# A hybrid decoder trunk on one Trainium2 core: score matmuls of sparse attention issued for both query tiles at once

## Chip, cores and metric

The kernel runs on one core of a Trainium2 chip. The metric is the device time of one execution in microseconds (us), as the median of several runs. One profiled execution gives the trace that is read below; its times count from the start of its span.

## What is computed

Input and output are 256 tokens by 1024 features, float32. The trunk has two layers. Each is a token mixer behind an RMS norm, a residual add, and a squared-ReLU MLP. The change concerns only the mixer of layer 1, native sparse attention with 16 heads in 4 groups of 4. It has three branches with keys and values of their own: compressed, selected blocks, sliding window. With 256 tokens every block is selected and the window holds the whole past, so the last two are plain causal attention. Cut to what matters:

```python
def nsa_mixer(h, w_in, cmp_pos_k, cmp_k_w1, cmp_k_w2, cmp_pos_v, ..., w_out):
    q, kc, vc, ks, vs, kw, vw, g = jnp.split(h @ w_in, cuts, axis=-1)
    kc = compress(kc, cmp_pos_k, cmp_k_w1, cmp_k_w2)   # 15 blocks: gelu(flat @ w1) @ w2
    vc = compress(vc, cmp_pos_v, cmp_v_w1, cmp_v_w2)
    ...
        pc = jax.nn.softmax(sc, axis=-1)     # compressed, sc = q.kc*scale - slope*dist
        ps = jax.nn.softmax(ss, axis=-1)     # selected
        pw = jax.nn.softmax(sw, axis=-1)     # window
        out = g0 * (pc @ vc) + g1 * (ps @ vs) + g2 * (pw @ vw)
    return out @ w_out
```

## The kernel before

All 256 tokens are two query tiles `t` of 128. A float32 projection is written as three products of rounded halves (`wh`/`wl` of the weights, `x1h`/`x1l` of the input): `fmajor_steps` issues 8 x 3 matmuls of the full 128x128 array into one PSUM bank, for the keys (`ps_k`), the queries of a group (`ps_q`) and the inputs of the compression (`ps_c`). ScalarE casts each weight block into `wh` (L66), VectorE forms `wl` (L69). The banks of these products, of transposes (`pt`, `ptc`) and of products with values (`o`) come from one set of four that is used in turn.

Score matmuls are smaller: `nsa_scores(g, t, b)` (L947) issues four, one for each head of group `g`, for one query tile and branch `b` (0 selected, 1 window), each on a 64x128 part of the array, into a tile `s` of two banks; there are two such tiles, and the compressed scores use them too. Behind each set of matmuls follows its softmax: VectorE adds the distances and takes the extreme (L964), ScalarE takes the exponential with its sum (L967), VectorE inverts and gates the sums (L969, L970), GpSimd scales (L972). `nsa_cmp_scores(g)` (L974) does the compressed branch of a group with eight small matmuls, its adds on VectorE at L987. `values(i)` transposes the probabilities of one group and tile; `products(i)` multiplies them by the values (`o`, parts of 128x64). `compress_hidden` (`ps_h`, also 128x64) and `compress_gelu` (copy `hc` at L886, then `ps_hT`) are the MLP of the compression.

The order is written as Python generators: `run(a, b)` steps through several of them in proportion, so that a set of scores falls between the steps of a projection. A scheduler then fixes the queue of each engine, with the order of the program as priority; on the chip each queue runs in order. The mixer goes: keys `ks`, queries of group 0, keys `kw` beside the scores (0, 0), compression input of the keys beside the scores (0, 1), that of the values, then queries, hidden layers and the scores (1, 0) and (1, 1), and then for each group and tile transposes, products, scores of the groups 2 and 3, and the projections that are left. Out of `kw` come the copies `kd` (L709 on ScalarE, L710 on VectorE), and out of `ps_c` the copies `fsk` and `fsv` (L866 and L868), four on each engine for each bank.

Of the kernel before, what the change touches and what calls it, by code (L numbers as in the profile page):

```python
# [85 lines left out]
class Trunk:  # L86
# [577 lines left out]
    def odd_mixer(self, xT, oT, pool, out):  # L664
        nc = self.nc

        v2 = pool.tile([P, 2, 2, NG * 64], F32, name="v2")

        gates = pool.tile([P, 3, 2, 16], F32, name="gates")

        kd = pool.tile([P, NG, KW], F32, name="kd")

        vc = pool.tile([P, NG, 2, 64], F32, name="vc")
        pc = [pool.tile([P, 2, 2, 2, 32], F32, name=f"pc{i}") for i in range(2)]
        self.nsa_constants(pool)
        nc.gpsimd.memset(kd[:, :, CW - 1 : CW], 0.0)
        nc.gpsimd.memset(vc, 0.0)
        for z in pc:
            nc.gpsimd.memset(z, 0.0)
        ws = self.W.get(("vs",))  # L680
        w0 = self.W.get(("vw", 0))
        w1 = self.W.get(("vw", 1))
        for t in range(2):
            if t:
                self.run_late()
            ps = self.bankB("ps_vs")
            self.tmajor(ps[:, :S], ws, xT, t, range(8), True, True)
            nc.scalar.copy(v2[:, t, 0, :], ps[:, :S])
            ps = self.bankB("ps_vw")
            self.tmajor(ps[:, :304], w0, xT, t, range(4), True, False)  # L690
            self.tmajor(ps[:, :304], w1, xT, t, range(4, 8), False, True)
            nc.vector.tensor_copy(v2[:, t, 1, :], ps[:, :S])
            ga = gates[:, :, t, :]
            nc.scalar.activation(ga, ps[:, 256:304].rearrange("p (h b) -> p b h", b=3), AF.Exp, scale=-1.0)
            nc.vector.tensor_scalar(ga, ga, 1.0, None, op0=ALU.add)
            nc.vector.reciprocal(ga, ga)
        g0 = gates[:, 0, 0, :]
        nc.vector.tensor_scalar(g0, g0, self.valid, None, op0=ALU.mult)

        def keys(key, off):  # L700
            yield 2 * KT
            w = self.W.get((key,))
            for m in range(2):
                ps = self.bankB("ps_k")
                yield from self.fmajor_steps(ps[:, :S], w, m, xT)
                for i in range(2):
                    src = ps[64 * i : 64 * i + 64, :S]
                    c = slice(off, off + S)
                    nc.scalar.copy(kd[64 * i : 64 * i + 64, 2 * m + i, c], src)  # L709
                    nc.vector.tensor_copy(kd[64 - 64 * i : 128 - 64 * i, 2 * m + i, c], src)  # L710
                yield 1

        with self.tc.tile_pool(name="nsa", bufs=1) as up, \
                self.tc.tile_pool(name="ps_nsa", bufs=2, space=PSUM) as banks:
            qs, p, parts = {}, {}, {}

            def queries(g):
                return self.nsa_queries(g, xT, qs, up)

            def scores(g, b):  # L720

                yield 2
                for t in range(2):
                    self.nsa_scores(g, t, b, qs, kd, gates, p, up, banks)
                    yield 1

            def cmp_scores(g):
                self.nsa_cmp_scores(g, qs, kd, gates, pc[g % 2], banks)

            order = [(g, t) for g in range(NG) for t in range(2)]  # L730

            def values(i):

                g, t = order[i]
                todo = self.nsa_transposes(g, t, p, pc[g % 2], parts, up)
                yield next(todo)
                for n, _ in enumerate(todo):
                    if n == 0 and i > 0:
                        products(i - 1)
                    yield 1  # L740

            def products(i):
                g, t = order[i]
                self.nsa_products(g, t, parts, oT, v2, vc)

            run(keys("ks", CW))
            run(queries(0))
            run(keys("kw", CW + S), scores(0, 0))
            f = [None, None]
            run(self.compress_blocks(0, xT, up, pool, f), scores(0, 1))  # L750
            run(self.compress_blocks(1, xT, up, pool, f))
            q1 = queries(1)
            next(q1)
            run(part(q1, KT))
            h = [self.bankB(f"ps_h{kv}") for kv in range(2)]
            run(self.compress_hidden(f[0], h[0]))
            hk = self.compress_gelu(0, h[0], up)
            run(part(q1, KT))
            run(self.compress_hidden(f[1], h[1]), scores(1, 0))
            hv = self.compress_gelu(1, h[1], up)  # L760
            self.compress_keys(hk, f[0], kd)
            q2 = queries(2)
            next(q2)
            run(part(q2, KT), scores(1, 1))
            self.compress_values(hv, f[1], vc)
            cmp_scores(0)
            run(part(q2, KT), values(0))
            cmp_scores(1)
            q3 = queries(3)
            next(q3)  # L770


            run(values(1), part(q3, 4))
            run(values(2), part(q3, 6), scores(2, 0))
            run(values(3), part(q3, 6), scores(2, 1))
            cmp_scores(2)
            rows = self.out_rows("odo", oT)
            next(values4 := values(4))
            run(part(values4, 1))
            run(part(values4, 2), part(rows, 2), scores(3, 0))  # L780
            run(values(5), part(rows, 2), scores(3, 1))
            cmp_scores(3)
            run(values(6), part(rows, 2))
            run(values(7), part(rows, 2))
            products(7)
            return out(banks)
# [155 lines left out]
    def nsa_scores(self, g, t, b, qs, kd, gates, p, pool, banks):  # L942


        nc = self.nc
        n = P * (t + 1)
        if t:  # L947
            o = self.scratch(pool, [P, 4, n], "p")
        else:
            if b == 0:  # L950
                p[g] = self.tmp.tile([P, 2, 4, n], F32, tag=("xg", "gain")[g % 2], name="p")
            o = p[g][:, b]
        p[g, t, b] = o
        nm = self.sm.tile([P, 4], F32, tag="nm", name="nm")
        sums = self.sm.tile([P, 4], F32, tag="sums", name="sums")
        c0 = CW + b * S
        ps = banks.tile([P, 1024], F32, tag="s2", name=f"s{g}{t}{b}")
        z = [ps[:, h % 2 * 512 + h // 2 * n : h % 2 * 512 + h // 2 * n + n] for h in range(4)]
        for h in range(4):
            d = slice(64 * (h % 2), 64 * (h % 2) + 64)  # L960
            self.mm(z[h], qs[g][d, h // 2, t * P : (t + 1) * P], kd[d, g, c0 : c0 + n], True, True,
                    skip_group_check=True)
        for h in range(4):
            nc.vector.tensor_tensor_reduce(out=o[:, h], in0=z[h], in1=self.dist[:, 2 * P - n : 2 * P], op0=ALU.add,  # L964
                                           op1=ALU.min, scale=-self.slope(4 * g + h), scalar=BIG,
                                           accum_out=nm[:, h : h + 1])
            nc.scalar.activation(o[:, h], o[:, h], AF.Exp, bias=nm[:, h : h + 1], scale=-1.0,  # L967
                                 accum_out=sums[:, h : h + 1])
        nc.vector.reciprocal(sums, sums)  # L969
        nc.vector.tensor_mul(sums, sums, gates[:, 1 + b, t, 4 * g : 4 * g + 4])  # L970
        for h in range(4):
            nc.gpsimd.tensor_scalar(o[:, h], o[:, h], sums[:, h : h + 1], 0.0, op0=ALU.mult, op1=ALU.add)  # L972

    def nsa_cmp_scores(self, g, qs, kd, gates, pc, banks):  # L974
# [3 lines left out]
        for t in range(2):  # L978
            for a in range(2):
                for r in range(2):  # L980
                    d = slice(64 * r, 64 * r + 64)
                    i = 2 * t + a
                    self.mm(ps[:, r, i * CW : (i + 1) * CW], qs[g][d, a, t * P : (t + 1) * P], kd[d, g, :CW], True, True,
                            skip_group_check=True)
        for t in range(2):
            dist = self.dist[:, 2 * P + t * CW : 2 * P + (t + 1) * CW]
            nc.vector.tensor_add(pc[:, t, :, :, :CW], ps[:, :, 2 * t * CW : 2 * (t + 1) * CW].rearrange("p r (a c) -> p r a c", a=2),  # L987
                                 bass.AP(tensor=dist.tensor, offset=dist.offset, ap=[dist.ap[0], [0, 2], [0, 2], [1, CW]]))
# [171 lines left out]
```

## Time and profile before

| what | value |
|---|---|
| median of 3 runs (666.63, 667.12, 1045.58) | 667.12 us |
| profiled execution, its own time | 669.41 us |
| its span, from first to last instruction | 667.7 us |
| mean granted TensorE clock in it | 0.985 |
| busy share: TensorE, VectorE, ScalarE, GpSimd | 97, 61, 52, 7 % |

The mixer of layer 1 takes the stretch from about 345 to 475 us. In the timeline each line is one instruction, or several alike in a row (xN): its start, its time, engine, line, operation, the tile it writes and those it reads, and in brackets how long the engine had been idle before it and which instruction of which engine released it. A float32 matmul of the scores runs in two passes, so four of them are x8. The array part of a matmul stands before its shape: 128*128 is the full array. Matmuls overlap, so the pitch from one start to the next is what one costs, not its own time.

### The profile page before, as it was taken

The page shows a single profiled execution, that of the slowest core. Times are in us where ns is not written, and L with a number is a line of the kernel's source. Part 1 is how long each engine was busy: PE and PEld are TensorE (multiplying, and loading weights), DVE is VectorE, ACT ScalarE, POOL GpSimd, SP SyncE. Part 2 cuts the span into 40 slices and gives each one's busy share as a digit, 9 for nine tenths or more (in the row PEclk, how much of TensorE's full clock was granted, in tenths as well). Part 3 has the DMA queues.
Part 4 walks back from the last instruction along what each step waited for, and adds up shares of the span by engine and source line. Part 5 has one row for each costly group of instructions (what it writes and reads, how often), then busy time and mean ns, then how long its engine had stood idle before and what let it go on. Part 6 is the DMA issues. An engine that isn't in the chain of part 4 may idle for free.

```text
span 667.7 us, 11136 instructions
## 1 busy us (share of the span) xinstructions
PE 647.5 (97%) x4257; PEld 566.6 (85%) x4257; DVE 408.4 (61%) x820; ACT 346.7 (52%) x699; POOL 46.3 (7%) x139
## 2 busy tenths in 40 slices
PE   6899999999999999999999989999999999999995
PEld 3798898889989898988898878777899899998984
DVE  5854637886555555555877485776775555555534
ACT  5565556555444444444567464753554445454423
POOL 3200000000000000000203321430000000000000
PEclk7999899999999999999999999999999999999998
DMA  7784243346555555555597632023365555656601
GB/s 255 229 261 138 71 149 127 116 156 212 188 183 189 182 182 183 184 186 143 155 319 243 194 110 64 1 64 124 110 222 180 188 188 190 189 190 185 192 2 63
DMA packets 74277, 108.67 MB, mean 163 GB/s; under 512 B 5072, under 2 KB 60400, under 8 KB 74224
## 3 DMA queue, kind: packets, MB, share of 16 engines
q1 hardware_dynamic: 74224, 107.97, 50.6%
q8 instruction: 33, 0.54, 0.3%
q14 instruction: 20, 0.16, 0.1%
HBM read 106.91 MB, written 1.05 MB: 162 GB/s over the span
## 4 chain that ended last, share of the span: by engine, by line
PE 90%; DVE 5%; ACT 2%; issue 1%; DMA 1%; SPq 0%; ACTq 0%; DVEq 0%
PE macc L108 26%; PE ps_up L108 24%; PE ps_f L108 7%; PE acc L108 4%; PE ps_q L108 4%; PE ps_ut L108 3%; PE ps_v L108 3%; PE o L108 2%; PE s L108 2%; PE z L108 2%; PE ps_or L108 2%; PE ps_k L108 2%; PE pt L1015 2%; DVE wl L69 1%; PE ps_h L108 1%
## 5 line engine op out<-in xcount | busy, mean ns | idle before, releaser
L69 DVE TENSOR_TENSOR wl<-w,wh 128x1024 fp32r<-128x1024 f32 (+1 forms) x188 | 225.1, 1214 | 176.8 <-ACT wh L66 176.5
L66 ACT CAST wh<-w 128x1024 fp32r<-128x1024 f32 (+1 forms) x190 | 192.9, 1040 | 176.0 <-PE macc L108 83.3
L108 PE MATMUL macc<-wh,l 128*128 128x512 f32 x256 | 101.2, 395 | 0.0
L108 PE MATMUL macc<-wh,h 128*128 128x512 f32 x256 | 101.1, 395 | 0.0
L108 PE MATMUL macc<-wl,h 128*128 128x512 f32 x256 | 101.0, 394 | 0.0
L108 PE MATMUL ps_up<-m0h,wh 128*128 128x256 f32 x224 | 63.4, 283 | 0.0
L108 PE MATMUL ps_up<-m1h,wh 128*128 128x256 f32 x224 | 63.4, 283 | 0.0
L108 PE MATMUL ps_up<-m0h,wl 128*128 128x256 f32 x224 | 63.3, 283 | 0.0
L108 PE MATMUL ps_up<-m1h,wl 128*128 128x256 f32 x224 | 63.3, 283 | 0.0
L108 PE MATMUL ps_up<-m1l,wh 128*128 128x256 f32 x224 | 63.3, 283 | 0.0
L108 PE MATMUL ps_up<-m0l,wh 128*128 128x256 f32 x224 | 63.3, 283 | 0.0
L108 PEld LDWEIGHTS macc<-wh,l 128*128 128x128 f32 x256 | 48.2, 188 | 11.2
L108 PEld LDWEIGHTS macc<-wh,h 128*128 128x128 f32 x256 | 48.4, 189 | 10.0
L108 PEld LDWEIGHTS macc<-wl,h 128*128 128x128 f32 x256 | 48.3, 188 | 10.0
L108 PEld LDWEIGHTS ps_up<-m0l,wh 128*128 128x128 f32 x224 | 42.9, 191 | 0.6
L108 PEld LDWEIGHTS ps_up<-m1l,wh 128*128 128x128 f32 x224 | 42.8, 191 | 0.6
L108 PEld LDWEIGHTS ps_up<-m0h,wh 128*128 128x128 f32 x224 | 42.8, 191 | 0.6
L108 PEld LDWEIGHTS ps_up<-m1h,wh 128*128 128x128 f32 x224 | 42.8, 191 | 0.6
L108 PEld LDWEIGHTS ps_up<-m1h,wl 128*128 128x128 f32 x224 | 42.9, 191 | 0.0
L108 PEld LDWEIGHTS ps_up<-m0h,wl 128*128 128x128 f32 x224 | 42.9, 191 | 0.0
L972 POOL TENSOR_SCALAR p<-p,sums 128x128 f32<-128x128 f32 (+1 forms) x64 | 31.4, 508 | 80.5 <-ACT kd L709 25.9
L108 PE MATMUL ps_f<-x0h,wh 128*128 128x256 f32 x128 | 36.4, 285 | 0.0
(285 smaller groups left out, 1202.9 us busy)
## 6 DMA issues: line engine op xcount, KB each, us to landing
w<-in_mlp_w_dram SPq DMA_DIRECT2D x128, 512.0 KB, 4.3
w<-in_ev_w_in_dram SPq DMA_DIRECT2D x24, 512.0 KB, 4.9
w<-in_od_w_in_dram SPq DMA_DIRECT2D x18, 512.0 KB, 5.3
w<-in_ev_w_out_dram SPq DMA_DIRECT2D x8, 512.0 KB, 4.3
w<-in_od_w_out_dram SPq DMA_DIRECT2D x8, 512.0 KB, 3.6
cwk<-in_od_cmp_k_w_dram SPq DMA_DIRECT2D x8, 256.0 KB, 6.0
cwv<-in_od_cmp_v_w_dram SPq DMA_DIRECT2D x8, 256.0 KB, 5.7
w<-in_od_w_in_dram SPq DMA_DIRECT2D x4, 304.0 KB, 3.0
```

What stands on the lines that cost most here:

```text
L66: self.nc.scalar.copy(wh[:, c], w)
L69: eng.tensor_sub(wl[:, c], w, wh[:, c].bitcast(F32))
L108: self.nc.tensor.matmul(out, lhsT, rhs, start=start, stop=stop, **kw)
L972: nc.gpsimd.tensor_scalar(o[:, h], o[:, h], sums[:, h : h + 1], 0.0, op0=ALU.mult, op1=ALU.add)
L1015: nc.tensor.transpose(pt[:, h * P : (h + 1) * P], p[g, t, b][:, h, kt * P : (kt + 1) * P], self.ident)
```

## The change

The generators `nsa_scores` and `nsa_cmp_scores` now stop once (a `yield`) after their matmuls. `scores(g, b)` issues the matmuls of both query tiles together and returns the two softmaxes, which `soft()` then runs one after the other. In the first part `once()` puts this in the middle of the keys `kw` and in the middle of the compression input; scores (1, 0) stand behind the hidden layer of the compressed values and (1, 1) with the compressed scores of group 0 behind the first half of the third query projection. From there on `values(i, ...)` issues the scores that it is given right behind the products of the step before. The number of matmuls, their shapes, the softmax and the data stay as they were.

```diff
             def scores(g, b):
-                yield 2
-                for t in range(2):
-                    self.nsa_scores(g, t, b, qs, kd, gates, p, up, banks)
+                todo = [self.nsa_scores(g, t, b, qs, kd, gates, p, up, banks) for t in range(2)]
+                for f in todo:
+                    next(f)
+                return todo
+            def cmp_scores(g):
+                todo = self.nsa_cmp_scores(g, qs, kd, gates, pc[g % 2], banks)
+                next(todo)
+                return [todo]
+            def soft(todo):
+                for f in todo:
+                    for _ in f:
+                        pass
+            def once(f, n=3):
+                yield n
+                for i in range(n):
+                    if i == n // 2:
+                        f()
                     yield 1
...
-            def values(i):
+            def values(i, *scores):
...
                 for n, _ in enumerate(todo):
-                    if n == 0 and i > 0:
-                        products(i - 1)
+                    if n == 0:
+                        if i > 0:
+                            products(i - 1)
+                        for f in scores:
+                            soft(f())
                     yield 1
...
-            run(keys("kw", CW + S), scores(0, 0))
+            run(keys("kw", CW + S), once(lambda: soft(scores(0, 0))))
...
-            run(self.compress_blocks(0, xT, up, pool, f), scores(0, 1))
+            run(self.compress_blocks(0, xT, up, pool, f), once(lambda: soft(scores(0, 1))))
...
-            run(self.compress_hidden(f[1], h[1]), scores(1, 0))
+            run(self.compress_hidden(f[1], h[1]))
+            soft(scores(1, 0))
...
-            run(part(q2, KT), scores(1, 1))
+            run(part(q2, KT))
+            soft(cmp_scores(0))
+            soft(scores(1, 1))
             self.compress_values(hv, f[1], vc)
-            cmp_scores(0)
             run(part(q2, KT), values(0))
-            cmp_scores(1)
...
-            run(values(1), part(q3, 4))
-            run(values(2), part(q3, 6), scores(2, 0))
-            run(values(3), part(q3, 6), scores(2, 1))
-            cmp_scores(2)
+            run(values(1, lambda: cmp_scores(1)), part(q3, 4))
+            run(values(2, lambda: scores(2, 0)), part(q3, 6))
+            run(values(3, lambda: scores(2, 1)), part(q3, 6))
             rows = self.out_rows("odo", oT)
-            next(values4 := values(4))
-            run(part(values4, 1))
-            run(part(values4, 2), part(rows, 2), scores(3, 0))
-            run(values(5), part(rows, 2), scores(3, 1))
-            cmp_scores(3)
+            run(values(4, lambda: cmp_scores(2), lambda: scores(3, 0)), part(rows, 2))
+            run(values(5, lambda: cmp_scores(3), lambda: scores(3, 1)), part(rows, 2))
...
             self.mm(z[h], qs[g][d, h // 2, t * P : (t + 1) * P], kd[d, g, c0 : c0 + n], True, True,
                     skip_group_check=True)
+        yield 1
```

The first place is VectorE's queue while the first compression input is copied out of its bank: `ps_c_3892` is that bank, `s011` the window scores of group 0, tile 1, `wl58` the weights of the last query projection, and `ps_c_3968` (now) the bank filled after it. Before:

```order
L868 COPY fsk0_3874<-ps_c_3892 64x8x15
L970 TENSOR_TENSOR sums_3897<-sums_3897,gates_3395 128x4
L868 COPY fsk1_3875<-ps_c_3892 64x8x15
L964 ISA p_3950,nm_3951<-s011_3953,dist_195 128x256
L964 ISA nm_3951 128x1
L868 COPY fsk0_3874<-ps_c_3892 64x8x15
L964 ISA p_3950,nm_3951<-s011_3953,dist_195 128x256
L964 ISA nm_3951 128x1
L964 ISA p_3950,nm_3951<-s011_3953,dist_195 128x256
L964 ISA nm_3951 128x1
L868 COPY fsk1_3875<-ps_c_3892 64x8x15
```

Now:

```order
L985 RECIPROCAL sums_3920<-sums_3920 128x4
L883 COPY fsk0_3874<-ps_c_3892 64x8x15
L986 TENSOR_TENSOR sums_3920<-sums_3920,gates_3395 128x4
L69 TENSOR_TENSOR wl58_4284<-w58_4036,wh58_4283 128x1024
L883 COPY fsk1_3875<-ps_c_3892 64x8x15
L883 COPY fsk0_3874<-ps_c_3968 64x8x15
L69 TENSOR_TENSOR wl58_4284<-w58_4038,wh58_4283 128x1024
L883 COPY fsk0_3874<-ps_c_3892 64x8x15
L883 COPY fsk1_3875<-ps_c_3968 64x8x15
L883 COPY fsk1_3875<-ps_c_3892 64x8x15
```

The inversion of tile 1's sums (`sums_3920`), all but the end of the softmax of both tiles, now stands ahead of every copy out of `ps_c_3892`, and the last of these copies has both weight blocks of `wl58` and two copies of the next bank in front of it.

The second place is TensorE's queue at the end of the hidden layer of the compressed values (`ps_h1`), where `s101` are the window scores of group 1, tile 0. Before:

```order
L108 MATMUL ps_h1_4144<-cwv30_4018,fsv0_4022 64x256
L108 MATMUL ps_h1_4144<-cwv31_4020,fsv1_4023 64x256
L108 MATMUL s101_4299<-kd_3396,qs_4106 128x128 x3
L108 MATMUL ps_hT_4262<-fold_3440,hc_4260 128x64 x2
L108 MATMUL ps_co_4278<-gel_4166,w2k_3855 128x60 x2
L108 MATMUL ps_q_4293<-x1h_1515,wh57_4107 128x256
```

Now:

```order
L108 MATMUL ps_h1_4144<-cwv30_4018,fsv0_4022 64x256
L108 MATMUL ps_h1_4144<-cwv31_4020,fsv1_4023 64x256
L108 MATMUL ps_hT_4262<-fold_3440,hc_4260 128x64 x2
L108 MATMUL ps_co_4278<-gel_4166,w2k_3855 128x60 x2
L108 MATMUL ps_q_4293<-x1h_1515,wh57_4107 128x256
L108 MATMUL ps_q_4293<-x1l_1516,wh57_4107 128x256
```

The scores that stood between the hidden layer and the product `ps_hT` are gone from here; they stand behind the first half of the query projection.

The third place is TensorE's queue in the middle part, at the products of group 1, tile 0 (`o10`), where `s201` and `s211` are the window scores of group 2 for tiles 0 and 1. Before:

```order
L1015 MATMUL pt110_4619<-ident_88,p_4232 128x128 x4
L108 MATMUL o10_4626<-pT_4529,v2_3394 64x256 x2
L108 MATMUL o10_4626<-pT_4577,v2_3394 64x256 x2
L108 MATMUL o10_4626<-pcT_4610,vc_3397 64x256 x2
L108 MATMUL ps_q_4612<-x1h_1515,wh58_4283 128x256
L108 MATMUL ps_q_4612<-x1l_1516,wh58_4283 128x256
L108 MATMUL ps_q_4612<-x1h_1515,wl58_4284 128x256
L108 MATMUL s201_4640<-kd_3396,qs_4282 128x128 x4
L108 MATMUL ps_q_4612<-x1h_1515,wh58_4283 128x256
```

Now:

```order
L1032 MATMUL pt110_4619<-ident_88,p_4224 128x128 x4
L108 MATMUL o10_4626<-pT_4529,v2_3394 64x256 x2
L108 MATMUL o10_4626<-pT_4599,v2_3394 64x256 x2
L108 MATMUL o10_4626<-pcT_4610,vc_3397 64x256 x2
L108 MATMUL s201_4637<-kd_3396,qs_4282 128x128 x4
L108 MATMUL s211_4645<-kd_3396,qs_4282 128x256 x4
L108 MATMUL ps_q_4612<-x1h_1515,wh58_4283 128x256
```

The scores of tile 0 moved up against the products, and those of tile 1, which stood 12 rows further down between transposes, follow them at once.

## Rows read from the trace of the kernel before

**Rows 1.** Page, parts 1 and 4: engines; chain that ended last, by engine.

```profile
PE 647.5 (97%) x4257; PEld 566.6 (85%) x4257; DVE 408.4 (61%) x820; ACT 346.7 (52%) x699; POOL 46.3 (7%) x139
...
PE 90%; DVE 5%; ACT 2%; issue 1%; DMA 1%; SPq 0%; ACTq 0%; DVEq 0%
```

**Rows 2.** Stretches: length, busy PE, PEld, DVE, ACT, POOL, clock, DMA share, GB/s.

```profile
345.00:375.00 30.00, 29.61 (x238) 27.33 (x237) 22.39 (x65) 22.29 (x62) 9.56 (x16) 1.00 0.71 222
375.00:395.00 20.00, 17.43 (x137) 13.65 (x136) 11.55 (x37) 10.43 (x36) 2.71 (x7) 1.00 0.58 182
395.00:462.00 67.00, 67.00 (x528) 52.25 (x530) 46.22 (x178) 38.50 (x120) 20.26 (x46) 1.00 0.16 50
```

**Rows 3.** TensorE timeline: start us, us, operation, count; scores inside ps_c.

```profile
360.15 0.28 PE L108 MATMUL ps_c<-x1h,wl 128*128 128x256 f32 x1
360.36 0.72 PE L108 MATMUL s<-kd,qs 64*128 64x128 f32 x8
...
361.23 0.28 PE L108 MATMUL ps_c<-x1l,wh 128*128 128x256 f32 x1
```

**Rows 4.** TensorE timeline: scores ahead of ps_q, and ahead of values' products.

```profile
396.31 0.48 PE L108 MATMUL s<-kd,qs 64*128 64x128 f32 x2
396.73 0.39 PE L108 MATMUL ps_q<-x1h,wh 128*128 128x256 f32 x1
...
414.50 0.48 PE L108 MATMUL s<-kd,qs 64*128 64x128 f32 x2
414.92 1.95 PE L108 MATMUL o<-pT,v 128*64 128x256 f32 x16
```

**Rows 5.** Groups 345 to 475, ACT then DVE: busy us, mean ns, idle before.

```profile
L967 ACT ACTIVATE p<-p,nm 128x256 f32<-128x256 f32 x32 | 15.9, 498 | 5.6 <-DVE nm L964 5.5
L967 ACT ACTIVATE p<-p,nm 128x128 f32<-128x128 f32 x32 | 12.5, 392 | 7.4 <-DVE nm L964 7.4
...
L69 DVE TENSOR_TENSOR wl<-w,wh 128x1024 fp32r<-128x1024 f32 x21 | 25.6, 1231 | 5.5 <-ACT wh L66 5.5
```

**Rows 6.** VectorE timeline: two softmax starts, copies out of ps_c.

```profile
353.80 0.29 DVE L964 CUSTOM_DVE_ANT_0 p<-s,dist 128x128 f32<-128x128 f32 x1
...
362.61 0.29 DVE L964 CUSTOM_DVE_ANT_0 p<-s,dist 128x128 f32<-128x128 f32 x1
...
367.87 0.29 DVE L868 COPY fsk<-ps_c 64x120 f32<-64x120 f32 x1
...
373.98 0.28 DVE L868 COPY fsk<-ps_c 64x120 f32<-64x120 f32 x1 [0.32 <-ACT fsk L866]
```

**Rows 7.** ScalarE timeline: kw key copy, first copy out of ps_c.

```profile
355.69 0.35 ACT L709 COPY kd<-ps_k 64x256 f32<-64x256 f32 x1
...
363.91 0.25 ACT L866 COPY fsk<-ps_c 64x120 f32<-64x120 f32 x1
```

**Rows 8.** TensorE timeline: the bank of the first ps_c reused; next ps_q.

```profile
370.87 0.28 PE L108 MATMUL ps_c<-x1h,wl 128*128 128x256 f32 x1
370.99 0.28 PE L108 MATMUL ps_c<-x1h,wh 128*128 128x256 f32 x1
...
374.41 0.36 PE L108 MATMUL ps_q<-x1h,wh 128*128 128x256 f32 x1 [0.39 <-DVE fsk L868]
```

**Rows 9.** TensorE timeline: end of ps_h and the products behind it.

```profile
394.19 0.71 PE L108 MATMUL s<-kd,qs 64*128 64x128 f32 x6
394.87 0.66 PE L108 MATMUL ps_hT<-fold,hc 128*128 128x64 f32 x4
```

**Rows 10.** ScalarE timeline: the copy that the product ps_hT reads.

```profile
394.47 0.35 ACT L886 COPY hc<-ps_h 128x256 f32<-128x256 f32 x1
```

**Rows 11.** Two early stretches, columns as in the stretches above.

```profile
9.00:19.00 10.00, 8.09 (x22) 6.12 (x23) 9.57 (x12) 6.38 (x10) 4.14 (x2) 0.50 0.83 290
64.00:70.00 6.00, 6.00 (x18) 4.51 (x19) 2.18 (x5) 3.85 (x6) 0.00 (x0) 0.50 0.14 48
```

**Rows 12.** TensorE timeline: its longest wait, in front of that stretch.

```profile
10.33 1.08 PE L286 MATMUL ps_t<-ident,xg 128*128 128x128 f32 x4 [4.01 <-DVE xg L309]
```

More of the change, by code (lines that the diff above doesn't have):

```diff
@@ L720, in scores @@
             def scores(g, b):
-                yield 2
-                for t in range(2):
-                    self.nsa_scores(g, t, b, qs, kd, gates, p, up, banks)
+                todo = [self.nsa_scores(g, t, b, qs, kd, gates, p, up, banks) for t in range(2)]
[15 more added lines that the diff above has]
+                        f()
                     yield 1
-            def cmp_scores(g):
-                self.nsa_cmp_scores(g, qs, kd, gates, pc[g % 2], banks)
             order = [(g, t) for g in range(NG) for t in range(2)]
-            def values(i):
+            def values(i, *scores):
                 g, t = order[i]
@@ L984, in nsa_cmp_scores @@
                             skip_group_check=True)
+        yield 1
         for t in range(2):
```

## The prediction

> **What bounds the kernel now.** I read the page first. TensorE is busy 97% of the span, the chain that ended last runs on it for 90%, and no other engine passes 61% [rows 1]. So what counts is how long TensorE takes for its queue and where that queue waits. Then the stretches of the mixer. From 345 to 375 us TensorE has 0.39 us without work, from 375 to 395 it has 2.57 us, and from 395 to 462 none, all at the full granted clock of 1.00, 2.4 GHz [rows 2]. The idle time lies where hidden layer, queries and scores follow one another one by one. The bunched scores run mostly in the full last stretch: there only fewer or cheaper TensorE instructions can gain, and only a new wait can lose. In the first stretch VectorE and ScalarE are busy 22.4 and 22.3 of 30 us, so a different order on them can reach TensorE.
>
> Last I read TensorE's timeline for what an excursion to the scores costs. With scores inside `ps_c`, the start of the second product after them is 1.08 us later than that of the last product before them [rows 3]. A product's pitch is 0.12, from 370.87 to 370.99 [rows 8], so two steps are 0.24. Two heads use the two halves of the array's rows side by side; one score alone (x2) takes 0.48 [rows 4] and four (x8) take 0.72 [rows 3], so I take 0.24 for a pair of heads and 0.48 for four scores. What is left, 1.08 - 0.24 - 0.48 = 0.36, is the price of leaving the full array and coming back, 0.18 for each change of the array part. A score in front of `ps_q` hands over after 0.42 us, and one in front of the products with values after 0.42 too [rows 4]: a change from the scores' part to the values' part costs what a change to the full array costs.
>
> **The change, part by part.** *Fewer changes of array part.* I counted changes between full array, scores' part and values' part along the two TensorE queues from the first key projection of this mixer to its out-projection: 67 before, 48 now. Six of the 19 go in the front, where the scores of group 0 stood four times apart in the key projection and the compression input. Thirteen go behind the hidden layers. At `o10`, for instance, the order of parts was full, values, full, scores, full, scores, full; now it is full, values, scores, full. At 0.18 that is 1.08 us in the front and 2.34 us behind it. The Trainium skill, "TensorEngine Tiling (Array Packing)", Key Properties, says that a change of tiling mode drains TensorE; putting scores beside products with values, which have another tiling, would by that rule still pay. The 0.42 of both hand-overs agrees, so the count takes such a neighbour as a change like any other.
>
> *A later softmax in the front.* The matmuls cost the same, but both softmaxes now stand together, ahead of the copies that empty the bank of the first `ps_c` (first place in the order). I walked ScalarE and VectorE along by durations of the trace. For the scores (0, 0), one more weight subtraction of 1.23 us [rows 5] stands ahead of the first adds, which start at 355.0 instead of 353.80 [rows 6]. Four exponentials of 128 columns at 0.39 and four of 256 at 0.50 [rows 5] follow, from 355.4 to 359.0. Only then come the key copies, the first of which started at 355.69 [rows 7]: about 3.2 us later. Behind them wait two casts and two subtractions of 1.23; idle time before and between them takes up some of the delay. So the adds of (0, 1) start near 364.55 instead of 362.61 [rows 6], the exponentials end near 368.45, and the first copy out of `ps_c` starts there instead of at 363.91 [rows 7]. Eight copies on two engines empty that bank. Now the casts and subtractions of `wl58` and copies of the next bank stand between them: on VectorE two subtractions, 2.46, six copies at 0.29, 1.74, and three hand-overs from ScalarE of about 0.3 as in the row at 373.98 [rows 6]. That is 5.1 us, so the last copy ends near 373.5. Before it ended at 367.87 + 0.29 = 368.16.
>
> *A new wait behind it.* The bank is needed again by the first `ps_c` of the compressed values. Before, TensorE came to it at 370.99, 2.8 us after the last copy, and went on without idle time [rows 8]. Now it arrives 1.08 earlier, at 369.9, and waits until 373.5: 3.6 us. Behind it in TensorE's queue are 24 products of this bank at 0.12, then `ps_q` of group 1, its hidden layers and all that follows. `ps_q` starts at 373.5 + 2.9 + 0.1 = 376.5 instead of 374.41; its own wait of 0.39 [rows 8] goes, because the copies of the next bank end before that. The front therefore loses 2.1, its gain of 1.08 included. The bounds: no wait at all, with `ps_q` as early as before less 0.4 to 1.1; and a wait that lasts 1.2 longer, which is one subtraction more ahead of the last copy: 3.3 later. I take 2.1, the result of the walk. What follows, query copy and first score, is a chain of TensorE and ScalarE and only shifts.
>
> *Scores gone from in front of `ps_hT`.* Before, three scores ran from 394.19, and `ps_hT` started at 394.87 [rows 9]. Under them ScalarE made the copy that `ps_hT` reads, from 394.47 to 394.82 [rows 10]. Now nothing stands between `ps_h` and `ps_hT` (second place). The same copy is now bare, 0.7 us from the end of `ps_h`, less the 0.1 that the first product would wait for its issue: a loss of 0.6. Bounds are 0.35, the copy alone, and 1.1, with one exponential of (1, 0) of 0.50 still ahead of it.
>
> *Softmaxes bunched in the middle.* A compressed set and two tiles of scores now share two score tiles, and VectorE works them off in turn. TensorE must wait for a tile that is not read yet, and transposes for a probability not yet scaled. By the durations above I find one place where this shows, the compressed transpose of group 2, about 0.3. In this stretch VectorE is busy 46 of 67 us [rows 2], which is cover, but not where three sets come at once. Bounds: 0, and 2.0, which is a set of four exponentials of 256 columns ahead of the awaited one, at 0.50 each [rows 5]. I take 0.3, near the end at which TensorE stands in the last row of [rows 2], without a wait.
>
> *Sum.* +2.1 (front) - 2.34 + 0.6 + 0.3 = +0.7 us. The profiled execution has 669.41, of which 667.7 are the span and the rest lies around it; it would become 670.1. The median of 667.12 lies 2.3 lower, and from it the forecast is 667.8 us.
>
> **The rivals.** *The wait stops the clock (slower).* Early in the span TensorE waited 4.01 us [rows 12]. In the stretch that begins inside that wait, 9 to 19, its granted clock was 0.50, that is 1.2 GHz, for 10 us; another stretch at 0.50 from 64 to 70 had no such long wait [rows 11]. Against it: 2.57 us idle in smaller pieces from 375 to 395 left the clock at 1.00 [rows 2]. Place: the wait ahead of the first `ps_c` of the compressed values. It decides from the point where that wait comes near 4 us. Price: half of the time spent at half clock, 3 us by the stretch of 6 us and 5 by that of 10. Time: 667.8 + 3 to + 5, so 670.8 to 672.8, take 671.5. The Trainium skill, "TensorE: Matmul & The Clock Gate", HAM oscillation, describes such a fall after waits for data, again at each of them. The row of the 4.01 us wait agrees; that a wait of 3.6 does it, no row here shows.
>
> *The bank is free in time (faster).* ScalarE and VectorE catch up, since both idle for some 7.6 of 30 us in the first stretch [rows 2]. Then the wait of 3.6 shrinks below 1, the front gains 0.4 instead of losing 2.1, and the sum is -0.4 - 2.34 + 0.9 = -1.8: 665.3; with the whole 1.08 it is 664.6. Against it: the copies stand in one fixed queue behind the exponentials.
>
> *The middle waits more.* Two score tiles for three sets: 2.0 instead of 0.3. Time: 667.8 + 1.7 = 669.5. For it: three sets at once at groups 2 and 3. Against it: TensorE has transposes and products in between.
>
> **How the numbers follow.** Forecast as summed, 0.45, own range 666.3 to 669.0. Bank free in time, 0.25, at 664.6 to 665.3. Middle waits more, 0.12, at 669.5. Clock falls, 0.18, at 670.8 to 672.8. The range takes in all but the upper part of the last, and 0.6 below the second for the size of the price of a change: 664.0 to 671.5. A measurement of this kernel can tell about 2% from no change, 13.3 us. No case comes near that: faster by more 0.01, the same 0.97, slower by more 0.02, the last for a clock that falls several times.
>
> **What would show it right or wrong.** Right: a wait of TensorE at `ps_c` for a VectorE copy `fsk`, 3 to 4 us long, near 370; `ps_q` of group 1 about 2 us later than 374.41; `ps_hT` with a wait of about 0.6 for ScalarE's `hc`; and from there to the out-projection a stretch shorter by about 2 us with all TensorE work full. Each change of array part gone is 0.18 less. Wrong: no wait at `ps_c` and a shorter stretch, which is the bank free in time; a granted clock of 0.50 between 370 and 385, which is the fall; or waits of score matmuls for VectorE's reads in the middle.

## The result, and the profile after

The changed kernel takes 671.81 us in the median of 6 runs (670.04 to 674.03), the kernel before 668.20 in the runs beside it. The ratio, which leaves out the one run of 1045.58 of the kernel before, is 1.0057, 95% interval 1.0035 to 1.0079: 3.6 us slower between the medians and 3.8 by the ratio, where 0.7 were forecast, and 0.3 above the top of the range. Part of the distance to the forecast time is no matter of the change: the kernel before has 668.20 here, 1.1 more than the 667.12 from which the forecast started. The profiled execution of the changed kernel has 674.03 us, its span is 672.3.

The page of the changed kernel, parts 1 and 4:

```profile
PE 647.6 (96%) x4257; PEld 568.1 (84%) x4257; DVE 406.8 (61%) x820; ACT 346.4 (52%) x699; POOL 44.8 (7%) x139
...
PE 86%; DVE 5%; ACT 5%; issue 2%; DMA 1%; SPq 0%; ACTq 0%; DVEq 0%
```

TensorE does the same work as in [rows 1] (647.6 us busy against 647.5), but the chain that ended last now runs on it for 86% instead of 90%: part of it passes through other engines. The same three stretches as in [rows 2]:

```profile
345.00:375.00 30.00, 25.90 (x216) 24.37 (x215) 22.29 (x65) 21.34 (x60) 8.44 (x16) 1.00 0.74 230
375.00:395.00 20.00, 17.48 (x126) 15.33 (x125) 7.68 (x17) 7.54 (x20) 1.13 (x4) 0.91 0.47 155
395.00:462.00 67.00, 66.05 (x537) 51.62 (x534) 45.80 (x195) 39.00 (x133) 21.49 (x48) 1.00 0.17 56
```

From 345 to 375 TensorE now lacks 4.1 us instead of 0.4, and from 375 to 395 the granted clock is 0.91 where it was 1.00. TensorE's waits between 345 and 475 us name the place (total, times, longest):

```profile
PE ps_c L108 <- DVE fsk L883: 4.1, 1, 4.1
...
PE ps_hT L108 <- ACT hc L901: 0.6, 1, 0.6
```

Both waits are new. TensorE's timeline shows what lies around them; the first line is the first key product of this mixer, the last the first accumulation of the out-projection:

```profile
340.47 0.28 PE L108 MATMUL ps_k<-x1h,wh 128*128 128x256 f32 x1
...
370.35 0.28 PE L108 MATMUL ps_c<-x1h,wl 128*128 128x256 f32 x1
374.74 0.36 PE L108 MATMUL ps_c<-x1h,wh 128*128 128x256 f32 x1 [4.10 <-DVE fsk L883]
...
375.35 0.42 PE L108 MATMUL ps_c<-x1l,wh 128*128 128x256 f32 x1
375.56 0.41 PE L108 MATMUL ps_c<-x1h,wl 128*128 128x256 f32 x1
...
378.55 0.31 PE L108 MATMUL ps_c<-x1l,wh 128*128 128x256 f32 x1
...
378.81 0.28 PE L108 MATMUL ps_c<-x1h,wh 128*128 128x256 f32 x1
...
379.17 0.28 PE L108 MATMUL ps_q<-x1h,wh 128*128 128x256 f32 x1
...
395.28 3.64 PE L108 MATMUL ps_h<-cwv,fsv 128*64 128x256 f32 x30
399.53 0.66 PE L108 MATMUL ps_hT<-fold,hc 128*128 128x64 f32 x4 [0.60 <-ACT hc L901]
...
467.03 0.50 PE L108 MATMUL acc<-wh,o1h 128*128 128x512 f32 x1
```

TensorE is idle for 4.10 us in front of the third `ps_c`, and soon behind the wait the pitch of the products is no longer 0.12 but 0.21 (375.35 to 375.56). Fifteen products run that way, from 375.35 to 378.55, 0.213 each; from 378.81 to 379.17 three fit into 0.36 again. The granted clock of that stretch, columns as in [rows 2], is 0.50, that is 1.2 GHz:

```profile
375.40:378.50 3.10, 3.10 (x16) 3.10 (x16) 0.09 (x1) 0.00 (x0) 0.00 (x0) 0.50 0.35 127
```

`ps_q` starts at 379.17, where [rows 8] had 374.41. For the other marks of the kernel before, three more lines of its trace:

```profile
339.82 0.28 PE L108 MATMUL ps_k<-x1h,wh 128*128 128x256 f32 x1
...
390.62 3.64 PE L108 MATMUL ps_h<-cwv,fsv 128*64 128x256 f32 x30
...
462.37 0.50 PE L108 MATMUL acc<-wh,o1h 128*128 128x512 f32 x1
```

From the first key product to `ps_q` it takes 38.70 us instead of 34.59, 4.11 more. From the x30 run of `ps_h` to the first accumulation it takes 71.75 in both: the 13 changes of array part that are gone there brought nothing in sum. Together, from first key product to first accumulation, 126.56 instead of 122.55, 4.0 more. (The other 0.65 of the difference between the two profiled executions lies ahead of the first key product, in code that is the same.)

### The profile page after: what moved, and what is told of

It reads as the page before. It is cut to its first block, busy times and chain, and to the rows that moved or that the text cites. A ratio compares the mean times of both kernels' runs of the same rounds, so it can differ in the third digit from the quotient of the medians.

```text
span 672.3 us, 11141 instructions
## 1 busy us (share of the span) xinstructions
PE 647.6 (96%) x4257; PEld 568.1 (84%) x4257; DVE 406.8 (61%) x820; ACT 346.4 (52%) x699; POOL 44.8 (7%) x139
## 4 chain that ended last, share of the span: by engine, by line
PE 86%; DVE 5%; ACT 5%; issue 2%; DMA 1%; SPq 0%; ACTq 0%; DVEq 0%
PE macc L108 26%; PE ps_up L108 24%; PE ps_f L108 7%; PE acc L108 4%; PE ps_q L108 3%; PE ps_ut L108 3%; PE ps_v L108 3%; PE o L108 2%; ACT p L983 2%; PE ps_or L108 2%; PE z L108 2%; DVE wl L69 2%; PE pt L1032 1%; ACT wh L66 1%; PE s L108 1%
## 5 line engine op out<-in xcount | busy, mean ns | idle before, releaser
L108 PE MATMUL ps_f<-x0l,wh 128*128 128x256 f32 x128 | 36.2, 283 | 0.0
```

The source lines that it names most:

```text
L108: self.nc.tensor.matmul(out, lhsT, rhs, start=start, stop=stop, **kw)
```

## The experiments

Three marks serve for all: first key product to `ps_q` (front), x30 run of `ps_h` to first accumulation (middle), and the ratio to the kernel before. Theory 1: the bank of the first `ps_c` is emptied late, because the softmaxes stand ahead of its copies, and the wait lowers the clock. Theory 2: the bunched scores of the middle cost the time.

**Front apart, middle bunched.** The helper `apart` issues matmuls and softmax of one tile after the other, as the kernel before did; all runs that need it use it.

```diff
-            run(keys("kw", CW + S), once(lambda: soft(scores(0, 0))))
+            run(keys("kw", CW + S), apart(0, 0))
...
-            run(self.compress_blocks(0, xT, up, pool, f), once(lambda: soft(scores(0, 1))))
+            run(self.compress_blocks(0, xT, up, pool, f), apart(0, 1))
```

> The front (scores of group 0) is as in the kernel before, the rest as in the changed kernel. Theory 1, the loss is the late emptying of the first ps_c bank: no wait of TensorE at ps_c, granted clock 1.00 from 375 to 395, ps_q of group 1 within 0.2 us of where it stood before. From ps_hT to the first out-projection accumulation 67.5 us as in the changed kernel, the wait at ps_hT still 0.6. The ratio to the kernel before is 1.000, within 0.3%. Theory 2, the bunched scores of the middle cost the time: the ratio stays near 1.005.

Measured: ratio 0.9997, interval 0.9977 to 1.0016. TensorE's timeline of this run:

```profile
339.78 0.28 PE L108 MATMUL ps_k<-x1h,wh 128*128 128x256 f32 x1
...
374.37 0.35 PE L108 MATMUL ps_q<-x1h,wh 128*128 128x256 f32 x1 [0.39 <-DVE fsk L890]
...
390.58 3.64 PE L108 MATMUL ps_h<-cwv,fsv 128*64 128x256 f32 x30
...
462.32 0.50 PE L108 MATMUL acc<-wh,o1h 128*128 128x512 f32 x1
```

The front is 34.59 as before, the middle 71.74 as in both kernels, the wait at `ps_hT` is 0.6. All of the loss goes with the front, and theory 2 falls: the bunched middle costs nothing in sum. It does not bring its forecast gain either.

**Front bunched, middle as before.**

```diff
-            run(self.compress_hidden(f[1], h[1]))
-            soft(scores(1, 0))
+            run(self.compress_hidden(f[1], h[1]), apart(1, 0))
...
-            run(values(2, lambda: scores(2, 0)), part(q3, 6))
+            run(values(2), part(q3, 6), apart(2, 0))
...
```

> Only the front of the change (scores of group 0 bunched), the rest as in the kernel before. Theory 1: the wait at ps_c is 4.1 us, the clock falls behind it for about 3.3 us, ps_q of group 1 stands 4.3 later than before, and the ratio is 1.005 to 1.0065. From ps_hT on as in the kernel before, 67.5 us to the first accumulation of the out-projection. Theory 2: the ratio is within 0.2% of 1.000.

Measured: ratio 1.0057, interval 1.0037 to 1.0078, the wait 4.1, the front 38.72 and the middle 71.7. The front alone is the whole change in time.

**Only one of the two sets bunched.** First only (0, 0), then only (0, 1), by one of the two edits of the first experiment each.

> The changed kernel with the scores (0, 1) apart again, so that only (0, 0) are bunched in the key projection. If both softmaxes must be late to make the wait (theory 1): the copies of the first ps_c bank end near 370, TensorE reaches the bank at 370.5 and waits under 0.3 us, clock 1.00, ratio 0.999 to 1.001. Rival, the delayed key copies alone do it: a wait of 2 us or more at ps_c, ratio 1.003 to 1.005.

> The changed kernel with the scores (0, 0) apart again, so that only (0, 1) are bunched in the compression input. By the queues the copies end about 2 us earlier than in the changed kernel: a wait near 2 us at ps_c. If the clock falls only behind a wait of the length of the changed kernel's, it stays at 1.00, ps_q stands 1 to 1.5 later than before and the ratio is 1.001 to 1.003. Rival, a wait of 2 us is enough for the fall: granted clock under 0.95 from 375 to 395 and a ratio of 1.004.

Measured: with only (0, 0) bunched 0.9998 (0.9976 to 1.0019), no wait at `ps_c`; `ps_q` waits 1.0 instead of 0.4. With only (0, 1) bunched 1.0075 (1.0046 to 1.0103), where the expectation for a full clock was 1.001 to 1.003. The wait was 3.2 instead of the 2 expected, and the clock fell: 0.95 from 375 to 395. TensorE's timeline of the latter:

```profile
373.66 0.54 PE L108 MATMUL ps_c<-x1h,wh 128*128 128x256 f32 x1 [3.16 <-DVE fsk L890]
374.00 0.42 PE L108 MATMUL ps_c<-x1l,wh 128*128 128x256 f32 x1
374.22 0.42 PE L108 MATMUL ps_c<-x1h,wl 128*128 128x256 f32 x1
```

So the late key copies add only about 1 us to the wait; what makes it is the softmax of (0, 1), which stands directly ahead of the copies. The front is 38.5 us here and 38.7 in the changed kernel: the wait is 0.9 shorter, but four changes of array part are back. That the ratio is above the changed kernel's is within the intervals.

**The wait made shorter.** Scores (0, 1) still together, but 2 of 24 steps into the compression input instead of half way; then the same with (0, 0) apart.

```diff
-                    if i == n // 2:
+                    if i == (n // 2 if n == 3 else 2):
...
-            run(self.compress_blocks(0, xT, up, pool, f), once(lambda: soft(scores(0, 1))))
+            run(self.compress_blocks(0, xT, up, pool, f), once(lambda: soft(scores(0, 1)), 24))
```

> The changed kernel with the scores (0, 1), still together, two matmul groups into the compression input instead of half way. In VectorE's queue the last copy out of the first ps_c bank then has one subtraction of wl58 in front of it instead of two, and no copies of the next bank: 1.25 + 0.6 earlier, a wait of about 2.2 at the third ps_c instead of 4.1. If only a wait of 3 us or more lowers the clock: 1.00 from 365 to 390, and a ratio of 1.001 to 1.003. Rival, 2 us are enough: some 14 products at a pitch of 0.21 behind the wait, ratio over 1.003.

> As the run before, and the scores (0, 0) apart again: by the 3.2 us that the wait lasted with only the second set bunched, less 1.9, a wait of about 1.3. Clock 1.00 by the first theory, ratio 1.000 to 1.002; the rival has the fall here too, ratio over 1.002.

Measured: 1.0008 (0.9985 to 1.0031) and 0.9996 (0.9976 to 1.0017). The wait at the third `ps_c` was 1.9 in the first and 0.2 in the second, which I had put at 1.3. TensorE's timeline of the first:

```profile
370.09 0.36 PE L108 MATMUL ps_c<-x1h,wh 128*128 128x256 f32 x1 [1.88 <-DVE fsk L883]
370.29 0.28 PE L108 MATMUL ps_c<-x1l,wh 128*128 128x256 f32 x1
370.40 0.28 PE L108 MATMUL ps_c<-x1h,wl 128*128 128x256 f32 x1
```

From the second product behind this wait the pitch is 0.11 to 0.12, and the granted clock from 365 to 385 is 1.00. So behind waits of 4.1 (two kernels) and 3.2 us products ran at half the clock for about 3 us, and behind 1.9 and 0.2 not at all. Where the copies stand in the queue sets the wait, and on the wait hangs whether the clock falls. What a wait between 1.9 and 3.2 us does was not measured; and with one trace for each kernel it is not shown that the clock falls in every execution.

**The second set behind the compression input.**

```diff
-            run(self.compress_blocks(0, xT, up, pool, f), once(lambda: soft(scores(0, 1))))
+            run(self.compress_blocks(0, xT, up, pool, f))
+            soft(scores(0, 1))
```

> The changed kernel, but the scores (0, 1), still together, are issued behind the compression input of the keys, so that the copies out of the first ps_c bank stand ahead of their softmax. Theory 1: no wait over 0.3 at the third ps_c, clock 1.00, ps_q of group 1 starts at 373.4 to 374.4 (before 374.41), ratio 0.998 to 1.000. Rival, the softmax delays the copies of the second bank and only moves the wait: a wait of 2 us or more at ps_q or at the fourth ps_c, ratio over 1.002.

Measured: 0.9966 (0.9950 to 0.9982), better than expected. There is no wait at `ps_c`, and the one at `ps_q` is gone too:

```profile
340.25 0.28 PE L108 MATMUL ps_k<-x1h,wh 128*128 128x256 f32 x1
...
372.95 0.28 PE L108 MATMUL ps_q<-x1h,wh 128*128 128x256 f32 x1
```

The front is 32.70, 1.9 less than before: 0.4 is the old wait at `ps_q`, and 1.5 falls to changes of array part. There are seven fewer here, 0.21 each: the second set now stands beside the small product `ps_pos`, which is on a part of its own. The same matmuls together, with the copies ahead of the softmax, gain in place of losing.

**The price of a change of array part.** The kernel before with each set of scores issued as two halves at two places.

```diff
-                yield 2
+                yield 4
                 for t in range(2):
-                    self.nsa_scores(g, t, b, qs, kd, gates, p, up, banks)
+                    f = self.nsa_scores(g, t, b, qs, kd, gates, p, up, banks)
+                    next(f)
+                    yield 1
+                    for _ in f:
+                        pass
                     yield 1
...
         for h in range(4):
+            if h == 2:
+                yield 1
```

> The kernel before, with every set of score matmuls issued in two halves at two places, so that TensorE changes its array part 88 times instead of 67: 6 more in the front, 15 more behind the hidden layers. If a change costs 0.18 us: 2.7 us more between the end of ps_h and the first out-projection accumulation (74.4 instead of 71.75 from the start of the x30 run of ps_h), the front 1.1 later less what its waits take up, ratio 1.004 to 1.006. Rival, the changes cost next to nothing, and the changed kernel's middle gained nothing for that reason: ratio 1.000, stretch 71.75 within 0.5.

Measured: 1.0035 (1.0017 to 1.0053), a little under the range. The two marks of the middle:

```profile
390.50 3.64 PE L108 MATMUL ps_h<-cwv,fsv 128*64 128x256 f32 x30
...
465.27 0.50 PE L108 MATMUL acc<-wh,o1h 128*128 128x512 f32 x1
```

That is 74.77, 3.0 more than before for 15 more changes: 0.20 each, or 0.18 if a wait of 0.3 at a compressed transpose (`ptc`), which the kernel before does not have, is taken off. The front is 1.3 longer for 6 more, 0.2 of it a longer wait at `ps_q`. The price was right; the rival that the changes cost nothing falls.

**The middle without the late softmax.** Front apart. First both edits below, then each alone: the softmax of each tile one step later than the last, between transposes (spread), and the matmuls of (1, 1) in front of `ps_hT` (cover).

```diff
+                late = []
                 for n, _ in enumerate(todo):
                     if n == 0:
...
                         for f in scores:
-                            soft(f())
+                            soft(late)
+                            late = f()
+                    elif late:
+                        soft([late.pop(0)])
                     yield 1
+                soft(late)
...
             soft(scores(1, 0))
+            s11 = scores(1, 1)
             hv = self.compress_gelu(1, h[1], up)
             self.compress_keys(hk, f[0], kd)
+            soft(s11)
...
-            soft(scores(1, 1))
```

> Front as before. In the middle the matmuls of both tiles stand together, but each softmax is issued one step later than the last, between transposes, and the scores (1, 1) stand in front of ps_hT. TensorE changes its array part 29 times behind ps_h instead of 49 (before) and 36 (changed kernel). If the late softmax is what ate the gain: 20 changes at 0.18, 3.6 us less than before from the start of the x30 run of ps_h to the first accumulation, 68.2 instead of 71.75, no wait at ps_hT, ratio 0.994 to 0.996. Rival, the gain of a change is not 0.18 in this stretch: 71 to 72, ratio 0.999 to 1.000.

> Front as before, matmuls of both tiles together, each softmax of the middle one step later than the last; the scores (1, 1) stay behind the query projection. 31 changes of array part behind ps_h against 36 in the changed kernel. If VectorE's late copies of the transposes ate the gain: 71.74 - 5 x 0.2 - 0.9 = 69.8 from the x30 run of ps_h to the first accumulation, the wait at ps_hT still 0.6, ratio 0.996 to 0.998. Rival, only the cover of ps_hT and the fewer changes counted: 70.7.

> Front as before, softmaxes of the middle bunched as in the changed kernel, but the matmuls of the scores (1, 1) in front of ps_hT. 32 changes of array part instead of 36, no wait at ps_hT: 71.74 - 0.6 - 4 x 0.2 = 70.3 from the x30 run of ps_h to the first accumulation, ratio 0.997 to 0.999. Rival, the wait only moves to the score tiles: 71.5.

Measured: both 0.9947 (0.9926 to 0.9968), spread alone 0.9970 (0.9951 to 0.9989), cover alone 0.9979 (0.9953 to 1.0005). The marks of the run with both:

```profile
389.94 3.64 PE L108 MATMUL ps_h<-cwv,fsv 128*64 128x256 f32 x30
...
458.78 0.50 PE L108 MATMUL acc<-wh,o1h 128*128 128x512 f32 x1
```

The middle is 68.84 with both, 70.2 with spread, 69.9 with cover, against 71.75. Spread gained 0.4 less than expected, cover 0.4 more. Of spread's 1.5 the five changes fewer are 1.0 at 0.20, so the later softmax itself brought about 0.5, half way between the expectation and its rival. With both, the gain is there: 2.9 us in the middle for 20 changes fewer than before. At 0.20 each it should be 4.0; about 1.1 of that is still given back in this version, and where is not shown.

**All three: second set behind the input, spread, cover.**

> The scores (0, 1) behind the compression input, each softmax of the middle one step later than the last, the scores (1, 1) in front of ps_hT: 41 changes of array part instead of 67. If both theories hold, 1 us from the front and 3.6 from the middle: ratio 0.992 to 0.995, about 664.5 where the kernel before has 668.5. Rival, the waits return elsewhere: 0.998 or more.

Measured: 0.9931, interval 0.9911 to 0.9950, 0.7% below the kernel before. Marks, then the page, part 4:

```profile
338.26 0.28 PE L108 MATMUL ps_k<-x1h,wh 128*128 128x256 f32 x1
...
387.07 3.64 PE L108 MATMUL ps_h<-cwv,fsv 128*64 128x256 f32 x30
...
455.93 0.50 PE L108 MATMUL acc<-wh,o1h 128*128 128x512 f32 x1
```

```profile
PE 91%; DVE 3%; ACT 3%; issue 1%; DMA 1%; SPq 0%; POOL 0%; DVEq 0%; ACTq 0%; POOLq 0%
```

The middle is 68.86 as in the run with both edits, the front gains 1.9 as in the run with the second set behind the input, and from first key product to first accumulation it takes 117.67 instead of 122.55. The chain is back on TensorE for 91%.

## Why the prediction was wrong

**The walk along the queues held.** In the changed kernel the adds of (0, 0) and (0, 1) start as below, the first copy out of `ps_c` on VectorE at 369.59, and the last four copies end at 374.88. VectorE, then ScalarE:

```profile
355.76 0.29 DVE L980 CUSTOM_DVE_ANT_0 p<-s,dist 128x128 f32<-128x128 f32 x1
...
365.32 0.29 DVE L980 CUSTOM_DVE_ANT_0 p<-s,dist 128x128 f32<-128x128 f32 x1
...
369.59 0.28 DVE L883 COPY fsk<-ps_c 64x120 f32<-64x120 f32 x1
...
372.30 1.34 DVE L69 TENSOR_TENSOR wl<-w,wh 128x1024 fp32r<-128x1024 f32 x1
373.68 1.20 DVE L883 COPY fsk<-ps_c 64x120 f32<-64x120 f32 x4
```

```profile
359.63 0.35 ACT L709 COPY kd<-ps_k 64x256 f32<-64x256 f32 x1
...
369.30 0.25 ACT L881 COPY fsk<-ps_c 64x120 f32<-64x120 f32 x1
```

Less the 0.65 that this execution was late from the start, the two sets of adds start at 355.1 and 364.7 (forecast 355.0 and 364.55), the first key copy at 359.0 (359.0) and the first copy out of `ps_c` on ScalarE at 368.65 (368.45). The wait was 4.10 instead of 3.6: from the first copy to the end of the wait I had put down 5.1, and it took 374.74 - 369.30 = 5.4. The second subtraction, at 372.30, was slower with 1.34, and four copies stand behind it in one row.

**The clock was the step that failed.** The forecast let the wait pass at full clock; the fall was the first rival, at 670.8 to 672.8, and it came. Fifteen products at 0.213 instead of 0.12 are 1.4 us. With those at both ends of the fall, the 24 products of this bank take 4.43 (374.74 to 379.17) instead of 24 x 0.12 = 2.88, so the clock cost 1.55: half of the rival's lower price of 3, since it was low for little over 3 us and not for 6 or 10. It also came sooner than the wait of near 4 us that I had named: behind 3.2 us too. The front's sum as it came out: 4.10 (wait) + 1.55 (clock) - 0.39 (old wait at `ps_q`) - 1.2 (six changes) = 4.06, near the 4.11 measured, against 2.1. (The six are right, but the scores of group 0 stood apart five times before, not four: one set was parted.) The Trainium skill, "TensorE: Matmul & The Clock Gate", HAM oscillation, describes a fall of the clock behind waits for data. The row at 374.74 agrees, though the wait there is for a bank to be emptied. I had held against the fall that 2.57 us of idle time from 375 to 395 left the clock alone. That is a sum of waits of under 1 us, and no answer for one of 3.6.

**`ps_hT` was right**: a wait of 0.60 for ScalarE's `hc`, as forecast.

**The middle's term for bunched softmaxes was mis-sized.** The price of a change, 0.18, was near the 0.20 measured. But -2.34 + 0.6 + 0.3 = -1.44 was forecast and 0.0 came. From first key product to first accumulation the terms of the forecast add up to +0.66, and the trace has +4.01. Of what lies between them the clock is 1.55, the longer wait 0.5 and the middle 1.44; the higher price of a change gives 0.1 back in the front. TensorE's timeline shows where some of the middle's 1.44 went; these waits are so short that the list of waits has none of them:

```profile
404.39 1.84 PE L108 MATMUL s<-kd,qs 64*128 64x128 f32 x16
406.16 1.10 PE L108 MATMUL ps_co<-w2v,hT 128*128 128x64 f32 x8
...
426.17 0.28 PE L108 MATMUL ps_q<-x1h,wl 128*128 128x256 f32 x1
426.56 0.66 PE L1032 MATMUL pt<-ident,p 128*128 128x128 f32 x4
...
428.59 1.58 PE L108 MATMUL s<-kd,qs 64*128 64x128 f32 x16
430.10 0.39 PE L108 MATMUL ps_q<-x1h,wh 128*128 128x256 f32 x1
```

The sixteen passes of (1, 1) behind the compressed scores of group 0 last 1.77 to the next start (404.39 to 406.16), the same set of (2, 1) lasts 1.51: 0.26, where I had found 0. The transpose at 426.56 starts 0.39 behind a product whose pitch is 0.12: 0.27. By the times it waits for a bank, and VectorE shows why:

```profile
425.48 0.42 DVE L980 CUSTOM_DVE_ANT_0 p<-s,dist 128x256 f32<-128x256 f32 x1
425.82 0.69 DVE L1035 COPY pT<-pt 128x512 f32<-128x512 f32 x1
```

The copy `pT` out of a transpose's bank runs only from 425.82 to 426.51, behind the adds of the next group's scores, and the transpose starts right after it. That is the front's mechanism at small scale. Three more such places, of 0.1 to 0.3 each by the same reading, stand between 432 and 453. The run with spread alone bears it out: of these four, 0.89 together, 0.07 is left there (0.3 of this gain is not in that run's time, and what takes it up is not shown). So about 1.15 in place of 0.3. What is left, 0.6 to 0.9 by the price of a change, is not settled in full, but the traces show two parts of it. Three single scores of group 2 stand alone in the changed kernel (at 417.37, 418.49 and 419.49), one in the kernel before (414.50); each holds TensorE for 0.41 to 0.42, and a pair does so for no more (430.87 to 431.29 in the kernel before), so that a parted pair takes this time twice. With cover alone no score of group 2 stands alone, which fits its gain of 0.4 more than expected. And fewer changes beside the narrow compressed scores save less: with a set x8 behind them (from 437.20) they take 1.54 where the two apart take 1.00 and 0.65, a saving of 0.11, while two sets of scores joined save 0.20 (1.51 for 0.65 and 1.06).

**The rivals.** "The bank is free in time" named what the run with the second set behind the input reached by another order; in the change itself the copies stood in one queue behind the exponentials, as held against it. "The middle waits more" came in part.

## What to carry to other kernels

When work is bunched on the engine that sets the end, walk the engines behind it: the gain of fewer changes (0.20 us each here) is only had if the copies that empty its PSUM banks stand ahead of the bunched work in their queues. Issue the matmuls together and the softmaxes later, one at a time. And price a new wait at the bound engine with what the clock does behind it: a wait of 4.1 us cost 5.65 here.

## What I had not expected

The same code ahead of the mixer differs between executions by as much as the change costs: the first key product starts at 335.91 us in one trace (cover alone) and at 340.47 in another (changed kernel). In the execution of the kernel with only the front bunched, the first key product starts at 337.63 us, before at 339.82, and the two early stretches of [rows 11], both at 0.50 there, read:

```profile
9.00:19.00 10.00, 7.93 (x30) 5.66 (x30) 9.60 (x12) 6.40 (x10) 4.24 (x2) 0.83 0.83 276
64.00:70.00 6.00, 6.00 (x30) 4.79 (x31) 2.36 (x5) 4.75 (x7) 0.00 (x0) 1.00 0.29 87
```

TensorE had the full clock for more of these two stretches in this execution, and it reached the mixer 2.2 us earlier. For this reason marks inside the trace told the kernels apart better than the times did. Whether it makes the whole spread of some 5 us between runs of one kernel is not shown.
